# Eleven of 22 gate and up tiles of a ConvGLU from seven products of quarters in place of eight

## The chip, the cores and the metric

The kernel runs on one core of a Trainium2 chip. The metric is the device time of one execution in microseconds; the median of three runs stands for the kernel. Engines are named as in the profile: PE is TensorE's matmul stream and PEld its weight loads, DVE is VectorE, ACT ScalarE, POOL GpSimd, and SP the SyncE queue that issues most of the loads.

## The reference

One encoder layer on 512 tokens of width 1024, all in float32: a mixer of window attention and dilated attention, a cross attention to 256 memory tokens, and a ConvGLU, each followed by a residual and a layer norm. The change lies in the ConvGLU alone:

```python
def conv_glu(h, w_gate, w_up, conv_w, conv_b, w_down):
    s = h.shape[1]
    g = h @ w_gate
    half = CONV_WIDTH // 2
    gp = jnp.pad(g, ((0, 0), (half, half), (0, 0)))
    g = sum(gp[:, j:j + s] * conv_w[j] for j in range(CONV_WIDTH)) + conv_b
    return (jax.nn.gelu(g, approximate=False) * (h @ w_up)) @ w_down
```

`h` is 512 x 1024, `w_gate` and `w_up` are 1024 x 2816, `w_down` is 2816 x 1024, and the convolution is three taps wide along the tokens.

## The kernel before

**Number format.** Every float32 operand of a large product is split into two parts that TensorE takes in one pass each: `hi`, a cast on ScalarE (L134), and `lo = raw - hi`, a subtraction on VectorE (L136). A product is three matmuls: hi by hi, hi by lo, lo by hi (`gemm_fm`, L168).

**Layout of the stage.** The tokens' stream after the second layer norm is turned by TensorE (`to_T`, L202) into `h2T`, a pair (hi, lo) of tiles with the 1024 features on the partitions in eight blocks of 128 and the 512 tokens along the free dimension; a block of 128 tokens is turned at a time. The 2816 features of gate and of up are 22 tiles of 128 (`NF`). For one tile f, `w_cols` (L142) loads a 512 KB slice of 128 weight columns on SP's queue into one of three `raw` buffers and splits it into one of six `hi` and one of six `lo` buffers; `gemm_fm` then runs eight blocks by three matmuls of 128 x 128 weights against 512 tokens, 24 matmuls into one PSUM bank. Gate goes into a `g` tile (two one-bank buffers), up into the first bank of an `s` tile (two two-bank buffers); two further one-bank tiles are `t` and `o`. These are all eight banks.

**Tail of a tile** (L1356 to L1365). The gate is scaled by the middle tap and given its bias (ScalarE, L1357), the two outer taps are added from PSUM shifted by one token (VectorE, L1358 and L1361), then Gelu (ScalarE, L1364) and the product with up out of PSUM (VectorE, L1365), which is stored as `act[:, f, :]`.

**Order.** In the entry (L1323 to L1343) tiles 0 and 1 are computed by halves of the tokens, 256 columns a matmul, around the last two transposes (`pre_gemm`), with TensorE's order written out by hand. From L1345 on, tiles 2 to 21 and the down products are ordered by the framework's scheduler, which sets the order of every engine's instructions when the kernel is built and may bring an instruction forward if its inputs are there. On the other engines it does so in the entry too. The instructions run in that fixed order on each engine.

**Down.** `down_ops` (L1389) splits `act[:, k, :]` into two of the twelve `x` buffers and a row block of `w_down` into a hi and a lo buffer; for each k and each of four token blocks six matmuls accumulate into eight banks.

**Tiles that the change touches outside this stage.** `rc` and `rsn` (L498, L499), 2 KB a partition each, hold the cosines and sines of the rotary embedding, which are last read long before the ConvGLU. The `gb` tag of the weight pool has two buffers of 4 KB a partition, used for the norms' gains.

Of the kernel before, what the change touches and what calls it, by code (L numbers as in the profile page):

```python
# [9 lines left out]
F32 = mybir.dt.float32  # L10
F32R = mybir.dt.float32r
I32 = mybir.dt.int32
AF = mybir.ActivationFunctionType
ALU = mybir.AluOpType
# [3 lines left out]
P = 128  # L18
D = 1024
S = 512  # L20
NB = S // P
KD = D // P
# [3 lines left out]
NF = DFF // P  # L26
# [22 lines left out]
]  # L49

MEM_AT = (2, 0)
WARM = (12, 3)
CI, CF, CS, CMA, CM1, CM3 = 0, 128, 129, 130, 514, 770
CW = 898
# [17 lines left out]
def hymba_layer(ctx: ExitStack, tc: tile.TileContext, A, cst_d, out):  # L72
    nc = tc.nc
    X = mybir.AxisListType.X

    def pool(name, bufs=1, side="left", space=None):
        kw = {} if space is None else {"space": space}
        if space is None:
            kw["side"] = side
        return tc.tile_pool(name=name, bufs=bufs, **kw)  # L80

    cpool = ctx.enter_context(pool("const", side="right"))
    wpool = ctx.enter_context(pool("weights", side="right"))
    spool = ctx.enter_context(pool("small", bufs=3, side="right"))
    xpool = ctx.enter_context(pool("x2k", side="right"))
    spool.tile([P, 32], F32, tag="sfill", bufs=1, name="sfill")
    dpool = ctx.enter_context(tc.tile_pool(name="scratch", bufs=1, space=DRAM))

    cst = cpool.tile([P, CW], F32, name="cst")
    ident = cst[:, CI : CI + P]  # L90
    mhalf = cpool.tile([P, 1], F32, name="mhalf")
# [47 lines left out]
    def wsplit(raw, shape, eng=None):  # L139
        return split(raw, shape, wpool, "hi", 6, wpool, "lo", 6, eng)  # L140

    def w_cols(w, c0, eng=None):  # L142
        raw = wpool.tile([P, KD, P], F32, tag="raw", bufs=3, name="raw")
        nc.sync.dma_start(raw, w.rearrange("(k p) f -> p k f", p=P)[:, :, c0 : c0 + P])
        return wsplit(raw, [P, KD, P], eng)
# [10 lines left out]
    def on_pe(ins):  # L156
        if pe["pin"]:
            pe["pin"] = False
            tc.keep_in_program_order(ins)

    def pin():

        pe["pin"] = True

    def mm(o, l, r, first, last):
        on_pe(nc.tensor.matmul(o, l, r, start=first, stop=last))  # L166

    def gemm_fm(ps, wt, T, c0, n):  # L168
        whi, wlo = wt
        thi, tlo = T  # L170
        for k in range(KD):
            mm(ps, whi[:, k, :], thi[:, k, c0 : c0 + n], k == 0, False)
            mm(ps, whi[:, k, :], tlo[:, k, c0 : c0 + n], False, False)
            mm(ps, wlo[:, k, :], thi[:, k, c0 : c0 + n], False, k == KD - 1)
# [18 lines left out]
    def ps_tile(tag, bufs, shape=None):  # L193
        return gpool.tile(shape or [P, 512], F32, tag=tag, bufs=bufs, name=tag)

    def g_tile():
        return ps_tile("g", 2)

    def s_tile():
        return ps_tile("s", 2, [P, 2, 512])  # L200

    def to_T(t, T, b):  # L202
        ps = s_tile()
        for i in range(KD):
            f = i % 4 * P
            on_pe(nc.tensor.transpose(ps[:, i // 4, f : f + P], t[:, i * P : (i + 1) * P], ident))  # L206
        for i in range(2):
            k = slice(4 * i, 4 * i + 4)
            src = ps[:, i, :].rearrange("p (k t) -> p k t", k=4)
            hi = T[0][:, k, b * P : (b + 1) * P]  # L210
            nc.scalar.copy(hi, src)
            nc.vector.tensor_tensor(T[1][:, k, b * P : (b + 1) * P], src, hi.bitcast(F32), ALU.subtract)

    mid = ExitStack()
    tpool = mid.enter_context(pool("tT"))
# [18 lines left out]
    h = [(oA, oB)[b // 2][:, 2 * (b % 2) : 2 * (b % 2) + 2, :].rearrange("p a f -> p (a f)") for b in range(NB)]  # L234
# [134 lines left out]
    with tc.manual_schedule(engines={nc.tensor.engine, nc.vector.engine, nc.scalar.engine}):  # L369
# [5 lines left out]
        def busy(n, ps=None):  # L375
            for _ in range(n):
                mm((spare if ps is None else ps)[:, 0:P], ones_t, ones_t, True, True)

        busy(WARM[0])
        gps = [g_tile(), g_tile()]  # L380
# [3 lines left out]
        for n in range(2):  # L384
            mm(bt[n], ones_t, rows[:, 1, n, :], True, True)
        busy(WARM[1])
        vps = [g_tile(), g_tile()]
        two = s_tile()
# [106 lines left out]
        hl(3, *all_k)  # L495
        spill(2)

        rc = cpool.tile([P, S], F32, name="rc")  # L498
        rsn = cpool.tile([P, S], F32, name="rsn")  # L499
        posi = zs[:, 0, :].bitcast(I32)  # L500
        nc.sync.dma_start(posi, A["positions"].partition_broadcast(P)[:, 0, :])
        ang = zs[:, 2, :]
# [429 lines left out]
    with tc.manual_schedule(engines={nc.tensor.engine}):  # L932
# [125 lines left out]
        for c in range(KD):  # L1058
            whi, wlo = w_cols(w_xk, c * P)
            done("B2")  # L1060
            ps = g_tile()
# [52 lines left out]
        for hf in range(2):  # L1114
            wts = load_win(hf * 512)
            for b in range(NB):
                ps = g_tile()
# [6 lines left out]
    h = [hp[b] for b in range(NB)]  # L1124
# [28 lines left out]
    def U_pair():  # L1153
        return (
            U.tile([P, KD, S], F32R, tag="Uhi", name="Uhi"),
            U.tile([P, KD, S], F32R, tag="Ulo", name="Ulo"),
        )
# [80 lines left out]
    pin()  # L1238
    with tc.manual_schedule(engines={nc.tensor.engine}):
        to_T(h[0], h1T, 0)  # L1240
        for hf in range(2):
            dil_add(3, hf, dil_mm(3, hf))
        layer_norm(h[3], g1, b1)
        to_T(h[1], h1T, 1)
        proj_xv(1, [ps_tile("t", 1), ps_tile("o", 1)])
        kv(0)
        to_T(h[2], h1T, 2)
        wq = [w_cols(w_xq, c * P) for c in range(4)]
        part = [g_tile(), g_tile(), ps_tile("t", 1)]
# [50 lines left out]
        h2T = U_pair()  # L1300
# [16 lines left out]
    fp = ctx.enter_context(pool("ffn"))  # L1317
# [2 lines left out]
    nc.scalar.dma_start(cw[66:88, :], A["conv_b"][0].rearrange("(c p) -> c p", p=P))  # L1320
    cwT = fp.tile([P, 128], F32, name="cwT")[:, 0:88]
    act = fp.tile([P, NF, S], F32, name="act")
    pre = {}  # L1323
    pin()
    with tc.manual_schedule(engines={nc.tensor.engine}):
        pre = [[None, ps_tile("t", 1)], [None, ps_tile("o", 1)], [None, g_tile()], [None, g_tile()]]

        def pre_gemm(i, s2):
            if s2 == 0:
                pre[i][0] = w_cols(A[("w_gate", "w_up")[i % 2]][0], i // 2 * P)  # L1330
            gemm_fm(pre[i][1][:, s2 * 256 : (s2 + 1) * 256], pre[i][0], h2T, s2 * 256, 256)

        to_T(h[2], h2T, 2)
        pre_gemm(0, 0)
        pre_gemm(1, 0)
        tp = s_tile()[:, 0, 0:88]
        nc.tensor.transpose(tp, cw, ident[0:88, 0:88])
        nc.vector.tensor_copy(cwT, tp)
        pre_gemm(2, 0)
        to_T(h[3], h2T, 3)  # L1340
        pre_gemm(3, 0)
        for i in range(4):
            pre_gemm(i, 1)  # L1343

    pin()  # L1345
    for f in range(NF):
        if f < 2:
            pg, pu = pre[2 * f][1], pre[2 * f + 1][1]
        else:
            wg = w_cols(A["w_gate"][0], f * P)  # L1350
            wu = w_cols(A["w_up"][0], f * P)
            pg = g_tile()
            pu = s_tile()[:, 0, :]
            gemm_fm(pg, wg, h2T, 0, S)
            gemm_fm(pu, wu, h2T, 0, S)
        c = fp.tile([P, S], F32, tag="c", bufs=3, name="c")  # L1356
        nc.scalar.activation(c, pg, AF.Identity, scale=cwT[:, 22 + f : 23 + f], bias=cwT[:, 66 + f : 67 + f])  # L1357
        nc.vector.scalar_tensor_tensor(  # L1358
            c[:, 1:S], pg[:, 0 : S - 1], cwT[:, f : f + 1], c[:, 1:S], ALU.mult, ALU.add
        )  # L1360
        nc.vector.scalar_tensor_tensor(  # L1361
            c[:, 0 : S - 1], pg[:, 1:S], cwT[:, 44 + f : 45 + f], c[:, 0 : S - 1], ALU.mult, ALU.add
        )
        nc.scalar.activation(c, c, AF.Gelu)  # L1364
        nc.vector.tensor_tensor(act[:, f, :], c, pu, ALU.mult)  # L1365
    g3, b3 = (wpool.tile([P, D], F32, tag="gb", bufs=2, name="gb3") for _ in range(2))
    nc.sync.dma_start(g3, A["ln3_g"][0].partition_broadcast(P))
    nc.sync.dma_start(b3, A["ln3_b"][0].partition_broadcast(P))
    with gs:
        acc = [[ps_tile("t", 1), ps_tile("o", 1)]]  # L1370
        for b in range(1, NB):
            two = s_tile() if b != 2 else None
# [16 lines left out]
        def down_ops(k):  # L1389
            w = w_rows(A["w_down"][0], k, 1, 0, D)  # L1390
            a = split(act[:, k, :], [P, S], xpool, "x", 12, xpool, "x", 12)
            return w, a

        for k in range(KO):
            w, a = down_ops(k)
# [48 lines left out]
```

## Time and profile before

| | |
|---|---|
| median of 3 runs | 916.28 us (915.74 to 916.54) |
| the profiled execution | 916.33 us |
| its span, first to last instruction | 914.6 us, so 1.7 us lie around it |
| granted TensorE clock | 0.998 of full speed |
| entry of the ConvGLU (tiles 0 and 1) | about 545 to 571.4 us of the span |
| tiles 2 to 21 | about 571.4 to 787.4 us |
| down products and last norm | about 787.4 to 914.6 us |
| DMA | 92.81 MB, 101 GB/s over the span |

Times in the profile are microseconds from the span's start. A group's row names the line, the engine, the operation, the tile written and the tiles read, and the shape; then the busy time, the mean duration of one in nanoseconds, and the time that the engine was idle just before them with what ended it. Matmuls overlap each other in the records, so the duration of one is longer than the distance from its start to the next one's. L166 is the helper that issues nearly every matmul, so that the tile's name tells the groups apart.

### The profile page before, as it was taken

The numbers are of one execution on the slowest core, as the hardware profiler recorded it, in microseconds if no ns is written. First come the engines' busy times: TensorE is split into PE (matmuls) and PEld (weight loads), VectorE is DVE, ScalarE is ACT, GpSimd is POOL, SyncE is SP. The second block draws the span as 40 slices with busy tenths as digits, with TensorE's granted clock in tenths as the row PEclk, the third lists the DMA queues.
The fourth block names the chain that finished last, engine by engine and source line by source line (L and its number), as shares of the span: only waits on it lengthen the run. The fifth ranks groups of instructions, "written<-read, shape, count | busy, mean of one in ns | idle before, by whom it ended". The sixth has DMA issues, their size and how long they took to land.

```text
span 914.6 us, 12181 instructions
## 1 busy us (share of the span) xinstructions
PE 903.1 (99%) x4809; PEld 760.0 (83%) x4809; DVE 497.2 (54%) x856; ACT 362.3 (40%) x636; POOL 127.5 (14%) x106
## 2 busy tenths in 40 slices
PE   9999999999999999999999999999999999999996
PEld 7778987898878898789988889888888888888885
DVE  7975146435446677778565595543344434333346
ACT  4564436415545476314553224432332333222210
POOL 1064034332444420010000010000000000000001
PEclk9999999999999999999999999999999999999999
DMA  6762041314222338316212314333333332223201
GB/s 218 227 209 72 22 138 48 87 52 116 70 70 58 98 105 249 116 47 184 77 64 68 108 44 150 116 99 108 93 92 92 101 107 92 92 93 98 86 24 70
DMA packets 116940, 92.81 MB, mean 101 GB/s; under 512 B 12472, under 2 KB 100752, under 8 KB 116882
## 3 DMA queue, kind: packets, MB, share of 16 engines
q1 hardware_dynamic: 116048, 89.80, 32.3%
q10 hardware_dynamic: 834, 2.22, 0.6%
q8 instruction: 38, 0.62, 0.3%
q14 instruction: 20, 0.16, 0.1%
HBM read 87.82 MB, written 4.19 MB: 101 GB/s over the span
## 4 chain that ended last, share of the span: by engine, by line
PE 95%; DVE 3%; DMA 1%; issue 0%; ACT 0%; POOL 0%; DVEq 0%; ACTq 0%
PE g L166 53%; PE s L166 27%; PE t L166 4%; PE o L166 4%; PE o L690 3%; PE s L678 2%; PE s L206 1%; DMA vt<-in_ln_in_g_dram 1%; PE s L1221 0%; DVE lo L277 0%; DVE oA L343 0%; DVE st L307 0%; DVE Tlo L362 0%; POOL zs L526 0%; DVE mx L1202 0%
## 5 line engine op out<-in xcount | busy, mean ns | idle before, releaser
L136 DVE TENSOR_TENSOR lo<-raw,hi 128x1024 fp32r<-128x1024 f32 x142 | 176.7, 1246 | 156.9 <-ACT hi L134 154.6
L134 ACT CAST hi<-raw 128x1024 fp32r<-128x1024 f32 x142 | 149.2, 1052 | 221.1 <-PE g L166 163.3
L166 PE MATMUL g<-Thi,hi 128*128 128x512 f32 x240 | 94.8, 395 | 0.0
L166 PE MATMUL g<-Tlo,hi 128*128 128x512 f32 x240 | 94.3, 393 | 0.0
L166 PE MATMUL g<-Thi,lo 128*128 128x512 f32 x240 | 94.0, 392 | 0.0
L166 PE MATMUL g<-Uhi,hi 128*128 128x512 f32 (+1 forms) x256 | 93.2, 364 | 0.0
L166 PE MATMUL g<-Uhi,lo 128*128 128x512 f32 (+1 forms) x256 | 92.8, 363 | 0.0
L166 PE MATMUL g<-Ulo,hi 128*128 128x512 f32 (+1 forms) x256 | 92.8, 363 | 0.0
L107 POOL TENSOR_TENSOR rs<-ve,mhalf 128x1 f32<-128x1 f32 x18 | 15.4, 854 | 530.0 <-DVE ve L113 521.8
L526 POOL TENSOR_TENSOR zs<-zs,rsn 128x512 f32<-128x512 f32 x29 | 59.3, 2046 | 147.1 <-DVE zs L525 147.1
L166 PE MATMUL g<-hi,Thi 128*128 128x512 f32 x184 | 71.6, 399 | 0.0
L166 PE MATMUL g<-hi,Tlo 128*128 128x512 f32 x184 | 71.0, 395 | 0.5 <-DVE Tlo L1169 0.5
L166 PE MATMUL g<-lo,Thi 128*128 128x512 f32 x184 | 70.6, 395 | 0.4 <-DVE lo L277 0.4
L166 PE MATMUL s<-Uhi,lo 128*128 128x512 f32 x160 | 62.3, 389 | 0.0
L166 PE MATMUL s<-Ulo,hi 128*128 128x512 f32 x160 | 62.3, 389 | 0.0
L166 PE MATMUL s<-Uhi,hi 128*128 128x512 f32 x160 | 62.2, 389 | 0.0
L524 DVE TENSOR_TENSOR zs<-g,rc 128x512 f32<-128x512 f32 x29 | 20.0, 688 | 68.1 <-PE g L166 31.5
L166 PEld LDWEIGHTS g<-Uhi,lo 128*128 128x128 f32 x256 | 48.3, 189 | 7.6
L166 PEld LDWEIGHTS g<-Uhi,hi 128*128 128x128 f32 x256 | 48.3, 189 | 7.4
L166 PEld LDWEIGHTS g<-Ulo,hi 128*128 128x128 f32 x256 | 48.2, 188 | 7.4
L166 PEld LDWEIGHTS g<-Thi,hi 128*128 128x128 f32 x240 | 45.1, 188 | 11.0 <-issue 0.9
L166 PEld LDWEIGHTS g<-Tlo,hi 128*128 128x128 f32 x240 | 45.1, 188 | 10.3 <-issue 1.4
(330 smaller groups left out, 1765.3 us busy)
## 6 DMA issues: line engine op xcount, KB each, us to landing
raw<-in_w_in_dram SPq DMA_DIRECT2D x37, 512.0 KB, 3.8
raw<-in_w_gate_dram SPq DMA_DIRECT2D x22, 512.0 KB, 3.8
raw<-in_w_up_dram SPq DMA_DIRECT2D x22, 512.0 KB, 3.9
raw<-in_w_down_dram SPq DMA_DIRECT2D x22, 512.0 KB, 3.3
raw<-in_w_xk_dram SPq DMA_DIRECT2D x8, 512.0 KB, 3.9
raw<-in_w_xv_dram SPq DMA_DIRECT2D x8, 512.0 KB, 3.3
raw<-in_w_xq_dram SPq DMA_DIRECT2D x8, 512.0 KB, 4.8
raw<-in_w_xo_dram SPq DMA_DIRECT2D x8, 512.0 KB, 3.3
```

The lines of the kernel that those rows point to most:

```text
L107: nc.gpsimd.tensor_tensor(out_, in_, mhalf, ALU.pow)
L134: nc.scalar.copy(hi, raw)
L136: (eng or nc.vector).tensor_tensor(lo, raw, hi.bitcast(F32), ALU.subtract)
L166: on_pe(nc.tensor.matmul(o, l, r, start=first, stop=last))
L206: on_pe(nc.tensor.transpose(ps[:, i // 4, f : f + P], t[:, i * P : (i + 1) * P], ident))
L524: nc.vector.tensor_tensor(zc, ps, rc, ALU.mult)
L526: nc.gpsimd.tensor_tensor(sh, sh, rsn, ALU.mult)
L678: nc.tensor.transpose(tp[:, k, :], s_, ident)
L690: nc.tensor.matmul(o[HJ[j], t0:t1], lhs(j), rhs(j), start=i == 0, stop=i == len(parts) - 1)
```

## The change

Take gate and up of one feature tile as a 2 x 2 block product. The weights are cut into four: the upper and lower half of the 1024 input features (four blocks of 128 each) of gate (`a11`, `a12`) and of up (`a21`, `a22`). The tokens' stream is cut into four: the same halves of the features by the left and right 256 tokens (`B11` to `B22`). Eight products of quarters make gate and up; Strassen's method in Winograd's form makes them from seven, with four sums of weight quarters (`s1` to `s4`, made anew for each tile), four sums of stream quarters (`T`, made once), and additions of the products behind them. The tiles in `SEVEN` are made in this way, the others as before. TensorE's order is written out by hand for all of tiles 0 to 21.

```diff
+SEVEN = (4, 5, 7, 8, 10, 11, 13, 14, 16, 17, 19)
...
+    rope = [cpool.tile([P, S], F32, tag="rope", bufs=2, name=n) for n in ("rc", "rsn")]
...
-    def to_T(t, T, b):
+    def to_T(t, T, b, raw=None):
...
+            if raw is not None:
+                nc.scalar.copy(raw[:, k, b * P : (b + 1) * P], src)
...
-        rc = cpool.tile([P, S], F32, name="rc")
-        rsn = cpool.tile([P, S], F32, name="rsn")
+        rc, rsn = rope
...
+    raw_u = act[:, NF - KD : NF, :]
...
-        to_T(h[2], h2T, 2)
+        to_T(h[2], h2T, 2, raw_u)
...
-        to_T(h[3], h2T, 3)
+        to_T(h[3], h2T, 3, raw_u)
...
+    def t_form(n, i, a, b):
+        k = slice(2 * i, 2 * i + 2)
+        r = act[:, 6 + 2 * n : 8 + 2 * n, :].rearrange("p a (b t) -> p (a b) t", t=HT)
+        nc.vector.tensor_tensor(r[:, k], a[:, k], b[:, k], ALU.subtract)
+        if n < 3:
+            hl = [xpool.tile([P, 2, HT], F32R, tag="x", bufs=12, name="x") for _ in range(2)]
+        else:
+            hl = [t4[:, 2 * i : 2 * i + 2, :], cpool.tile([P, 2, HT], F32R, tag="rope", bufs=2, name="t4l")]
+        nc.scalar.copy(hl[0], r[:, k])
+        nc.vector.tensor_tensor(hl[1], r[:, k], hl[0].bitcast(F32), ALU.subtract)
+        T.setdefault(n, []).append(hl)
+        T["raw", n] = r
+    def t_forms():
+        for r, q in ((R11, B11), (R21, B21)):
+            nc.vector.tensor_tensor(r, q[0].bitcast(F32), q[1].bitcast(F32), ALU.add)
+        for n, a, b in ((0, R12, R11), (2, R22, R12), (1, R22, 0), (3, R21, 1)):
+            for i in range(2):
+                t_form(n, i, a, b if n in (0, 2) else T["raw", b])
...
+    def product(ps, wt, u):
+        for k in range(HK):
+            for a, b in ((0, 0), (0, 1), (1, 0)):
+                mm(ps, wt[a][:, k, :], u(b, k), k + a + b == 0, k == HK - 1 and a == 1)
+    def parts(raw, n):
+        hi = wpool.tile([P, n, P], F32R, tag="hi", bufs=6, name="hi")
+        nc.scalar.copy(hi, raw)
+        lo = wpool.tile([P, n, P], F32R, tag="lo", bufs=6, name="lo")
+        nc.vector.tensor_tensor(lo, raw, hi.bitcast(F32), ALU.subtract)
+        return [[t[:, HK * i : HK * (i + 1), :] for t in (hi, lo)] for i in range(n // HK)]
+    def seven(f):
...
+        s13, s24 = (wpool.tile([P, KD, P], F32, tag="gb", bufs=2, name="gb") for _ in range(2))
...
+        A11, A12 = parts(raw[0], KD)
+        nc.vector.tensor_tensor(s1, a21, a22, ALU.add)
+        nc.vector.tensor_tensor(s3, a11, a21, ALU.subtract)
+        S1, S3 = parts(s13, KD)
+        nc.vector.tensor_tensor(s2, s1, a11, ALU.subtract)
+        nc.vector.tensor_tensor(s4, a12, s2, ALU.subtract)
+        S2, S4 = parts(s24, KD)
+        (A22,) = parts(a22, HK)
+        p1_ = ps_tile(("t", "o")[f % 2], 1)[:, sl]
+        product(p1_, A11, quarter(B11))
+        two = [g_tile(), g_tile(), s_tile()[:, 0, :]]
+        product(two[0][:, sl], A12, quarter(B21))
+        product(two[1][:, sl], S1, moving(0))
+        product(two[1][:, sr], S3, moving(2))
+        product(two[0][:, sr], S2, moving(1))
+        product(two[2][:, sl], S4, quarter(B22))
+        product(two[2][:, sr], A22, moving(3))
+        gu = fp.tile([P, 2 * S], F32, tag="gu", bufs=1, name="gu")
+        u34 = act[:, f, :]
...
+        nc.scalar.copy(gu[:, S + HT :], p1_)
+        nc.vector.tensor_tensor(pair(gu[:, 0:S]), pair(two[0]), twice(gu[:, S + HT :]), ALU.add)
+        nc.vector.tensor_tensor(pair(u34), pair(two[1]), twice(gu[:, sr]), ALU.add)
+        nc.vector.tensor_tensor(gu[:, S + HT :], two[1][:, sl], u34[:, sr], ALU.add)
+        nc.vector.tensor_tensor(gu[:, HT : S + HT], two[2], u34, ALU.add)
+        ffn_tail(f, gu[:, 0:S], gu[:, S:])
+    pin()
+    with tc.manual_schedule(engines={nc.tensor.engine}):
+        t_forms()
+        for f in range(2):
+            ffn_tail(f, pre[2 * f][1], pre[2 * f + 1][1])
+        for f in range(2, NF):
+            if f in SEVEN:
+                seven(f)
+                continue
...
+            gemm_fm(pg, wg, h2T, 0, S)
+            gemm_fm(pu, wu, h2T, 0, S)
+            ffn_tail(f, pg, pu)
```

`HT` is 256 tokens and `HK` four blocks of 128 features; `sl` and `sr` are the left and right half of 512 columns. `ffn_tail` is the tail of a tile as it was (L1356 to L1365), in a function. The raw right half of the stream is copied out of PSUM in `to_T` into tiles 14 to 21 of `act`, the left half is put together again as hi + lo, and the raw differences lie in tiles 6 to 13 of `act`; all of these are done with before the tiles are written. `gu`, 4 KB a partition with one buffer, holds gate and up of a changed tile for the tail. `moving` and `quarter` pick the hi or lo part of a difference or of a quarter of `h2T`.

More of the change, by code (lines that the diff above doesn't have):

```diff
@@ L1343, in hymba_layer, with ffn_tail @@
             pre_gemm(i, 1)
[L1345 to L1355, printed above, removed]
+    def ffn_tail(f, pg, pu):
         c = fp.tile([P, S], F32, tag="c", bufs=3, name="c")
@@ L1365, in hymba_layer @@
         nc.vector.tensor_tensor(act[:, f, :], c, pu, ALU.mult)
+    HT, HK = S // 2, KD // 2
+    sl, sr = slice(0, HT), slice(HT, S)
+    B11, B12, B21, B22 = (
+        [t[:, HK * i : HK * (i + 1), n] for t in h2T] for i in range(2) for n in (sl, sr)
+    )
+    R11, R12, R21, R22 = (raw_u[:, HK * i : HK * (i + 1), n] for i in range(2) for n in (sl, sr))
+    T = {}
+    t4 = fp.tile([P, HK, HT], F32R, name="t4")
+    def t_form(n, i, a, b):
[10 more added lines that the diff above has]
+        T["raw", n] = r
@@ new lines, in t_forms, with moving, quarter @@
+    def t_forms():
[4 more added lines that the diff above has]
+                t_form(n, i, a, b if n in (0, 2) else T["raw", b])
+    def moving(n):
+        return lambda w, k: T[n][k // 2][w][:, k % 2, :]
+    def quarter(q):
+        return lambda w, k: q[w][:, k, :]
+    def product(ps, wt, u):
+        for k in range(HK):
+            for a, b in ((0, 0), (0, 1), (1, 0)):
+                mm(ps, wt[a][:, k, :], u(b, k), k + a + b == 0, k == HK - 1 and a == 1)
@@ new lines, in parts, with twice, pair @@
+    def parts(raw, n):
[5 more added lines that the diff above has]
+    def seven(f):
+        raw = []
+        for name in ("w_gate", "w_up"):
+            raw.append(wpool.tile([P, KD, P], F32, tag="raw", bufs=3, name="raw"))
+            nc.sync.dma_start(raw[-1], A[name][0].rearrange("(k p) f -> p k f", p=P)[:, :, f * P : (f + 1) * P])
+        a11, a12, a21, a22 = (t[:, HK * i : HK * (i + 1), :] for t in raw for i in range(2))
+        s13, s24 = (wpool.tile([P, KD, P], F32, tag="gb", bufs=2, name="gb") for _ in range(2))
+        s1, s3, s2, s4 = (t[:, HK * i : HK * (i + 1), :] for t in (s13, s24) for i in range(2))
+        A11, A12 = parts(raw[0], KD)
[17 more added lines that the diff above has]
+        u34 = act[:, f, :]
+        def twice(v):
+            return v.unsqueeze(1).to_broadcast([P, 2, HT])
+        def pair(v):
+            return v.rearrange("p (a t) -> p a t", a=2)
+        nc.scalar.copy(gu[:, S + HT :], p1_)
[4 more added lines that the diff above has]
+        ffn_tail(f, gu[:, 0:S], gu[:, S:])
@@ new lines, in hymba_layer @@
+    pin()
[7 more added lines that the diff above has]
+                continue
+            wg = w_cols(A["w_gate"][0], f * P)
+            wu = w_cols(A["w_up"][0], f * P)
+            pg = g_tile()
+            pu = s_tile()[:, 0, :]
+            gemm_fm(pg, wg, h2T, 0, S)
+            gemm_fm(pu, wu, h2T, 0, S)
+            ffn_tail(f, pg, pu)
```

## The prediction

> **What bounds the kernel now.** I read the page's first part, then the chain that ended last, then the busy time by stage, then the groups of the gate and up stage, shapes kept apart.
>
> ```profile
> PE 903.1 (99%) x4809; PEld 760.0 (83%) x4809; DVE 497.2 (54%) x856; ACT 362.3 (40%) x636; POOL 127.5 (14%) x106
> PE 95%; DVE 3%; DMA 1%; issue 0%; ACT 0%; POOL 0%; DVEq 0%; ACTq 0%
> ```
>
> TensorE holds 95% of the chain. A busy PE is not yet PE at its limit, so the stage that the change rewrites has to be looked at by itself. Two rows of busy time, the first the stretch in which the last two half-width products of the entry run, the second the stage from about feature tile 4 to 21 (duration; busy PE, PEld, DVE, ACT, POOL with instruction counts; granted clock; DMA share; GB/s):
>
> ```profile
> 565.70:571.20 5.50, 5.50 (x48) 5.50 (x47) 4.28 (x6) 5.09 (x6) 0.00 (x0) 1.00 0.64 189
> 593.00:787.30 194.30, 194.30 (x859) 160.90 (x858) 83.31 (x93) 62.88 (x76) 0.00 (x0) 1.00 0.33 99
> ```
>
> In the second, TensorE has no idle time at all at a granted clock of 1.00, VectorE works 83.31 of 194.30 us, ScalarE 62.88. So a microsecond of matmul removed here is a microsecond of the kernel, as long as VectorE and ScalarE can carry what is put on them. What a matmul costs I take from the chain, since it gives the time of a whole run of back-to-back matmuls:
>
> ```profile
> 565.76 5.76 PE g L166 x48
> 571.52 6.15 PE s L166 x27
> 577.67 10.88 PE g L166 x48
> ...
> 596.93 5.44 PE s L166 x24
> 602.37 5.44 PE g L166 x24
> ```
>
> The first row is 48 matmuls of 256 columns (the second halves of feature tile 1's gate and up): 5.76/48 = 0.120 us each. The others have 512 columns: 5.44/24 = 0.2267 us each. Half the columns cost 53%, not 50%: 0.0133 us of each matmul does not shrink with its width. That is the whole price of Strassen's smaller blocks on TensorE.
>
> The groups' own durations must not be used for this:
>
> ```profile
> L166 PE MATMUL g<-Uhi,hi 128*128 128x512 f32 x192 | 74.8, 390 | 0.0
> L166 PE MATMUL g<-Uhi,hi 128*128 128x256 f32 x64 | 18.4, 287 | 0.0
> ```
>
> At 390 and 287 ns a tile would go from 48 x 0.390 = 18.7 us to 84 x 0.287 = 24.1 us; but 48 matmuls of 287 ns fit in 5.76 us only because they overlap, so these are latencies. The Trainium skill says the same of matmul rows ("Perfetto Trace Analysis", Identifying the Most-Contended Engine: pipelined matmuls make busy time a bad measure; the share of weight loading is the better one), and by that measure the half-width stretch is full, PEld 5.50 of 5.50 us, where the full-width stage has 160.90 of 194.30.
>
> **The change, TensorE.** An ordinary tile has gate and up, 2 x 24 matmuls of 512 columns: 2 x 5.44 = 10.88 us. A changed tile has seven products of 4 x 3 = 12 matmuls of 256 columns: 84 x 0.120 = 10.08 us. Difference 0.80 us, eleven times: **-8.8 us**. Seven eighths would have given 1.36 us per tile; the width takes 0.56 of it back.
>
> Here a rule stands beside the row. The Trainium skill ("TensorE: Matmul & The Clock Gate", Back-to-back issue gap) gives a warm gap of N/2.4 + 2.5 ns, 109.2 ns at 256 and 215.8 ns at 512 columns; by it a tile would save 48 x 0.2158 - 84 x 0.1092 = 1.19 us and the change 13.0 us. The trace has both widths in the same loop, at 0.120 and 0.2267 us, so I use 8.8.
>
> **VectorE and ScalarE per tile.** Groups of VectorE in the stage (busy us, mean ns, idle time before and what ended it), then one of the whole kernel for the 256-column shape, then ScalarE's of the whole kernel:
>
> ```profile
> L136 DVE TENSOR_TENSOR lo<-raw,hi 128x1024 fp32r<-128x1024 f32 x36 | 44.1, 1225 | 74.2 <-ACT hi L134 72.5
> L1361 DVE SCALAR_TENSOR_TENSOR c<-g,cwT,c 128x511 f32<-128x511 f32 x18 | 13.5, 750 | 0.6
> L1358 DVE SCALAR_TENSOR_TENSOR c<-g,cwT,c 128x511 f32<-128x511 f32 x18 | 13.4, 744 | 0.0
> L1365 DVE TENSOR_TENSOR act<-c,s 128x512 f32<-128x512 f32 x18 | 12.4, 688 | 33.6 <-PE s L166 33.6
> L136 DVE TENSOR_TENSOR lo<-act,hi 128x512 fp32r<-128x512 f32 x3 | 2.1, 685 | 0.7 <-ACT hi L134 0.7
> ```
> ```profile
> L905 DVE TENSOR_TENSOR x<-s,x 128x256 fp32r<-128x256 f32 x8 | 3.4, 419 | 1.8 <-ACT x L904 1.8
> ```
> ```profile
> L134 ACT CAST hi<-raw 128x1024 fp32r<-128x1024 f32 x142 | 149.2, 1052 | 221.1 <-PE g L166 163.3 <-PE s L166 26.8 <-issue 6.9
> L1357 ACT ACTIVATE c<-g,cwT 128x512 f32<-128x512 f32 x21 | 16.3, 777 | 0.0
> L1364 ACT ACTIVATE c<-c 128x512 f32<-128x512 f32 x22 | 13.9, 632 | 41.2 <-DVE c L1361 41.2
> L134 ACT CAST hi<-act 128x512 fp32r<-128x512 f32 x22 | 13.7, 622 | 63.4 <-PE s L166 62.4 <-DVE act L1365 1.0
> ...
> L1067 ACT COPY kmT<-g 128x256 f32<-128x256 f32 x8 | 2.9, 367 | 0.0
> ```
>
> An ordinary tile on VectorE: two lows 2 x 1.225, tail 0.744 + 0.750 + 0.688: **4.63 us**. A changed tile: four sums of quarters, 128x512, at 0.685 = 2.74; lows 3 x 1.225 + 0.685 = 4.36; the recombination, three of 512 and one of 256 out of PSUM, 3 x 0.688 + 0.419 = 2.48; the same tail, 2.18: **11.76 us**, more than the tile's 10.08 us of TensorE. On ScalarE it is 3 x 1.052 + 0.622 + 0.367 + 0.777 + 0.632 = 5.55 us, no bound.
>
> So VectorE is the question. The eleven tiles come in five pairs (4 5, 7 8, 10 11, 13 14, 16 17), each followed by an ordinary tile, and 19 alone. Over such a three VectorE has 2 x 11.76 + 4.63 = 28.2 us of durations, TensorE 2 x 10.08 + 10.88 = 31.04 us: 91%. It is less in truth, because starts are closer than durations:
>
> ```profile
> 563.92 1.23 DVE L136 TENSOR_TENSOR lo<-raw,hi 128x1024 fp32r<-128x1024 f32 x1 [5.96 <-ACT hi L134]
> ...
> 570.84 0.74 DVE L1358 SCALAR_TENSOR_TENSOR c<-g,cwT,c 128x511 f32<-128x511 f32 x1
> 571.50 0.68 DVE L136 TENSOR_TENSOR lo<-act,hi 128x512 fp32r<-128x512 f32 x1
> 572.10 0.74 DVE L1361 SCALAR_TENSOR_TENSOR c<-g,cwT,c 128x511 f32<-128x511 f32 x1
> 572.76 1.21 DVE L136 TENSOR_TENSOR lo<-raw,hi 128x1024 fp32r<-128x1024 f32 x1
> ```
>
> From 571.50 to 572.10 is 0.60 us for an instruction of 0.68; with some 0.08 us less on each of 16 instructions a changed tile is near 10.5 us and a three near 25 us, about 82%. It fits if VectorE forms weights ahead of the pair. Six hi and lo buffers serve: a changed tile takes four and frees the first after its second product. Counting through a three, every set can be formed 11 us or more before its product (the ordinary tile's gate set: freed at 8.64 us of the three, needed at 20.16). That is the cover under which I cost the eleven weight formations at nothing. Bounds: nothing at one end, at the other the full excess of an uncovered pair, 2 x (11.76 - 10.08) = 3.4 us. I take nothing, since the pitch row is the nearer one.
>
> The raw weights are the same bytes, two loads a tile on SP's queue, but each of the three raw buffers is held until the last sum of quarters has read it, and the next tile's load waits in SP's queue behind it. The latest load (a pair's second up tile) comes some 8 us ahead of its use; a load lands in:
>
> ```profile
> raw<-in_w_gate_dram SPq DMA_DIRECT2D x22, 512.0 KB, 3.8
> ```
>
> so that wait is covered too, cost nothing; without cover it would be 3.8 us once a pair.
>
> **PSUM and the single recombination buffer.** A changed tile holds both g buffers. Its first (products 2 and 5) is wanted by an ordinary tile 2.88 us after product 5 ends (products 6 and 7), by another changed tile 4.32 us after. Freeing it takes one 0.688 us add, and that needs the copy of product 1 in gu, which has one buffer: the tail of the changed tile before must be through. From that tile's end: 0.69 + 0.78 + 0.74 + 0.75 + 0.63 + 0.69 for the tail, 0.37 and 0.69 for copy and add, 5.3 us where 10.08 are there before the ordinary tile needs the buffer. Behind each waiting step VectorE's later weight formations queue, and behind the g buffer all of TensorE, whose order is now by hand. Four VectorE steps that each find a 1.23 us formation under way make 10.3 us: a stall of 0.2 us in each pair. Zero to 1.0 us in all, I take **+0.5**.
>
> **The entry.** New at the start are four PSUM copies, two sums of 1024, eight differences and eight lows of 512 and eight casts: on VectorE 2 x 1.225 + 16 x 0.685 = 13.4 us, from when the last transpose is split. The timeline above shows VectorE idle 5.96 us before 563.92, and seven(4) does not need them until some 24 us after tile 2's start; by themselves they are hidden. But they stand ahead of the tails of tiles 0 and 1, and tile 2's gate needs a g buffer that tile 1's tail frees. Before, the scheduler could run up tiles first (the chain's 27 s matmuls, then 48 g), and eight of them even earlier, from the first to the last of these rows but one:
>
> ```profile
> 558.10 0.40 PE L166 MATMUL s<-Uhi,hi 128*128 128x512 f32 x1
> ...
> 561.17 0.39 PE L166 MATMUL s<-Ulo,hi 128*128 128x512 f32 x1
> ...
> 571.36 0.40 PE L166 MATMUL s<-Uhi,lo 128*128 128x512 f32 x1
> ```
>
> By hand the gate comes first. Without these eight the entry ends at 571.36 - 8 x 0.2267 = 569.5 us, tile 1's gate at 566.8. Before, its buffer came free 4.2 us after the gate's end (568.6 to 572.10 + 0.74 = 572.84); at the same delay that is 571.0 now, a stall of 1.5 us.
>
> Ends: zero if the tail is prompt, 3.6 us if all 13.4 us go first. I take **+1.5**. Of the copies, one can stand in ScalarE's queue ahead of the second split of the last transpose:
>
> ```profile
> L211 ACT CAST Uhi<-s 128x512 fp32r<-128x512 f32 x16 | 9.3, 585 | 48.6 <-PE s L206 46.6 <-DVE Ulo L212 1.9
> ```
> ```profile
> 557.27 0.69 DVE L212 TENSOR_TENSOR Ulo<-s,Uhi 128x512 fp32r<-128x512 f32 x1 [0.65 <-ACT Uhi L211]
> ```
>
> That split ends at 557.96; 0.59 later is 558.55, and its four row blocks are read twelve half-width matmuls after 557.98, at 559.4. Cost nothing, at worst 0.6. None of these edits can give time below nothing: in this stage TensorE has no idle time to win back.
>
> **The exit.** All twelve x buffers hold differences until tile 19 is through, so the splits of act for the down stage cannot run early (before, the first was at 571.50). Two ordinary tiles, 21.8 us of TensorE, follow tile 19, and VectorE needs 9.3 us of them: cost nothing; without that cover one cast and low, 1.3 us, once.
>
> **Sum.** The profiled execution took 916.33 us (span 914.6), against the median of 916.28. 916.33 - 8.8 + 1.5 + 0.5 = **909.5 us**.
>
> **Rivals.** *No stall at all*: 907.5. For it, the idle VectorE of the stage; against it, the tile 2 gate. It is the low side of my case.
>
> *VectorE sets the pace in each pair.* Its order is fixed ahead and in order; where a recombination that waits for a product stands before the next tile's formations, nothing is formed ahead and the pair takes VectorE's 11.76 us a tile: 5 x 3.4 + 1.7 = 18.7 us of stalls more than TensorE's time, 916.33 - 8.8 + 1.5 + 18.7 = 927.7, slower. For it, the durations; against it, the pitch, and the ordinary tile's lows before, which waited for buffers, not for VectorE's turn (idle 74.2 us). It decides from 7.3 us of stalls in the pairs, 0.7 us a changed tile, and is clear from 9.1. Chance 0.15.
>
> *The cover holds in part*: 0.3 to 0.8 us of stall a changed tile on top of 909.0 (the sum without the 0.5), 912 to 918. Chance 0.22, half of it still clearly faster.
>
> *The narrow matmuls lose their fixed part*, 0.1133 us each, half of 0.2267: 1.36 us a tile, 15.0 in all, 916.33 - 15.0 + 2.0 = 903.3. The row of 48 matmuls speaks against it: 0.03. The Trainium skill's gap rule named above would lie between, at 905.3.
>
> *The entry blocks for its full 3.6 us*: 911.6, inside my case. That the change does not do what it says would show in the count of matmuls, which should grow by 11 x 36 = 396.
>
> **Chances.** About 0.2% (1.8 us) is what can be told from no change here: faster is below 914.5, slower above 918.1. My case (907 to 912) has 0.60, the cheaper narrow matmuls 0.03, half of the partial cover 0.11: faster 0.74. Same 0.11, slower 0.15. The range leaves out the pace-setting VectorE and the cheaper matmuls: 906.8 to 917.0.
>
> **What would show it.** Right: half-width products at 0.120 us start to start, changed tiles of 10.1 us in the chain, 5205 matmuls, VectorE over 80% busy in the stage, a gap of 1 to 3 us ahead of tile 2's gate, hardly any in the pairs. Wrong: TensorE waiting ahead of a g product on the recombination or the tail, or on a low of a weight sum; or a pitch off 0.120.

## The result, and the profile after

The changed kernel is slower, by 0.7%: **922.75 us** (922.01 to 923.18, 6 runs) against 916.29 us (915.74 to 916.68, 6 runs), ratio 1.007 with a 95% interval of 1.0057 to 1.0083. Forecast were 909.5 us and a range of 906.8 to 917.0.

The page's first part, then the shares of the chain that ended last:

```profile
span 921.1 us, 13178 instructions
PE 897.6 (97%) x5205; PEld 772.9 (84%) x5205; DVE 578.3 (63%) x984; ACT 392.0 (43%) x681; POOL 127.2 (14%) x106
PE 84%; DVE 9%; DMA 3%; issue 2%; ACT 1%; POOL 0%; SPq 0%; DVEq 0%; ACTq 0%
```

There are 396 more matmuls, as they should be, and TensorE is busy 5.5 us less. But its share of the chain fell from 95 to 84%, and VectorE's rose from 3 to 9%: TensorE now waits. The chain of the changed kernel (start, duration, group), from the layer norm behind the entry to the end of the first pair:

```profile
521.67 16.32 PE g L168 x72
544.27 2.35 DVE lo L138 x2
563.06 1.91 DVE act L1376 x4
578.88 7.32 PE g L168 x24
586.20 5.44 PE s L168 x24
...
602.51 1.43 PE t L168 x12
603.95 5.76 PE g L168 x48
609.71 2.88 PE s L168 x24
612.59 1.44 PE o L168 x12
614.03 5.76 PE g L168 x48
619.79 1.45 PE s L168 x12
623.10 5.73 PE g L168 x24
```

The products cost what was forecast: 48 half-width matmuls in 5.76 us, and tile 4 runs from 602.51 to 612.59, 10.08 us. The losses are around them: the chain leaves TensorE for VectorE from 544 to 578.88 us, tile 2's gate takes 7.32 us in place of 5.44, and the ordinary tile behind the pair starts at 623.10, though the pair's last matmul started at 622.38. The waits of TensorE name the rest (waiting instruction, releaser: us in total, times, longest):

```profile
PE g L168 <- DVE c L1355: 6.5, 1, 6.5
PE g L168 <- DVE gu L1447: 2.8, 5, 0.7
PE s L208 <- DVE h L126: 1.8, 1, 1.8
```

L1355 is the last tap of a tile's tail, here tile 1's; L1447 the add that frees a changed tile's first g buffer; L126 the layer norm ahead of the last transposes. Measured from start to start of the matmuls on either side, less their pace, these are 6.7, 3.6 (five of about 0.7) and 2.0 us.

A fourth loss is in no list of waits. TensorE's matmuls around the end of the long one:

```profile
578.88 0.77 PE L168 MATMUL g<-Uhi,hi 128*128 128x512 f32 x1 [6.51 <-DVE c L1355]
579.44 0.63 PE L168 MATMUL g<-Ulo,hi 128*128 128x512 f32 x1
579.87 0.63 PE L168 MATMUL g<-Uhi,lo 128*128 128x512 f32 x1
...
582.36 0.40 PE L168 MATMUL g<-Uhi,lo 128*128 128x512 f32 x1
582.59 0.40 PE L168 MATMUL g<-Uhi,hi 128*128 128x512 f32 x1
```

Behind the wait they start 0.43 us apart, and from 582.36 on 0.23 again: 3.48 us for eight starts that take 1.81 at full pace, 1.7 us lost. Busy time by stage shows why, in its clock column (third from the end), in the wait, behind it, after that, and, fourth, in one stretch of two changed tiles and an ordinary one:

```profile
572.00:578.80 6.80, 0.36 (x4) 0.16 (x2) 6.80 (x12) 2.96 (x3) 0.00 (x0) 0.75 0.27 77
578.80:582.50 3.70, 3.62 (x9) 2.94 (x10) 2.26 (x3) 0.63 (x1) 0.00 (x0) 0.53 0.18 45
582.50:590.00 7.50, 7.50 (x35) 6.17 (x34) 4.20 (x6) 1.73 (x2) 0.00 (x0) 1.00 0.16 48
...
623.10:654.89 31.79, 31.32 (x216) 29.21 (x216) 26.29 (x36) 14.63 (x19) 0.00 (x0) 1.00 0.35 100
```

The clock fell to about half while TensorE waited (0.75 is the mean of the whole wait), was still there for some 3.5 us behind it, and rose again. In the last row VectorE is busy 26.29 of 31.79 us, near the 25 that the prediction reckoned with: it is not the bound of this kernel.

Together: -8.8 + 2.0 + 6.7 + 1.7 + 3.6 = +5.2 us of the 6.5 measured. Of the other 1.3, 0.9 was there before the ConvGLU (the 72 matmuls at 521.67 us stood at 520.80). In the experiments' traces the same matmuls start anywhere from 519.98 to 522.46, in a part that the change leaves as it was; what shifts it was not tried. From these 72 matmuls to the last group of the chain that writes `t` (at 890.69 us before, 897.20 now), which leaves this shift out, the change costs 5.6 us.

**What held the tap.** VectorE's instructions in the entry of the changed kernel (start, duration):

```profile
548.88 1.22 DVE L1389 TENSOR_TENSOR act<-Uhi,Ulo 128x1024 f32<-128x1024 f32 x1
...
550.61 1.22 DVE L1389 TENSOR_TENSOR act<-Uhi,Ulo 128x1024 f32<-128x1024 f32 x1
551.74 0.69 DVE L131 BATCH_NORM_STATS2 st<-h 128x6 f32<-128x512 f32 x1
...
568.34 0.74 DVE L1352 SCALAR_TENSOR_TENSOR c<-t,cwT,c 128x511 f32<-128x511 f32 x1
...
572.53 0.74 DVE L1355 SCALAR_TENSOR_TENSOR c<-t,cwT,c 128x511 f32<-128x511 f32 x1
...
573.79 0.68 DVE L1421 TENSOR_TENSOR gb<-raw 128x512 f32<-128x512 f32 x1
574.40 1.21 DVE L1409 TENSOR_TENSOR lo<-raw,hi 128x1024 fp32r<-128x1024 f32 x1
575.53 0.68 DVE L1422 TENSOR_TENSOR gb<-raw 128x512 f32<-128x512 f32 x1
576.13 0.74 DVE L1352 SCALAR_TENSOR_TENSOR c<-g,cwT,c 128x511 f32<-128x511 f32 x1
...
577.39 0.68 DVE L1424 TENSOR_TENSOR gb<-gb,raw 128x512 f32<-128x512 f32 x1
577.99 0.74 DVE L1355 SCALAR_TENSOR_TENSOR c<-g,cwT,c 128x511 f32<-128x511 f32 x1
```

Both sums of the left half (L1389) need only the first two blocks of the stream, and the scheduler put them ahead of the last block's layer norm (L131 and what follows): 2.4 us of VectorE, 2.0 us of TensorE. Then the differences and lows of the quarter sums, and behind them sums and lows of tile 4's weights (L1421 to L1424), needed some 25 us later, stand ahead of tile 1's taps (L1352 at 576.13, L1355 at 577.99). These four instructions take 2.9 us from start to start (573.79 to 576.13 and 577.39 to 577.99); an estimate from these rows is that the quarter sums alone would have made a wait of some 3.8 us.

### The profile page after: what moved, and what is told of

Same layout as the page of the kernel before. It is cut to its first block, busy times and chain, and to the rows that moved or that the text cites. A ratio compares the mean times of both kernels' runs of the same rounds, so it can differ in the third digit from the quotient of the medians.

```text
span 921.1 us, 13178 instructions
## 1 busy us (share of the span) xinstructions
PE 897.6 (97%) x5205; PEld 772.9 (84%) x5205; DVE 578.3 (63%) x984; ACT 392.0 (43%) x681; POOL 127.2 (14%) x106
## 4 chain that ended last, share of the span: by engine, by line
PE 84%; DVE 9%; DMA 3%; issue 2%; ACT 1%; POOL 0%; SPq 0%; DVEq 0%; ACTq 0%
PE g L168 49%; PE s L168 20%; PE t L168 5%; PE o L168 4%; PE o L693 3%; PE s L681 2%; DMA raw<-in_w_mix_out_dram 2%; DVE lo L138 1%; DMA raw<-in_w_up_dram 1%; DVE lo L1409 1%; PE s L208 1%; DMA vt<-in_ln_in_g_dram 1%; ACT hi L136 1%; DVE Ulo L214 1%; DVE act L1376 0%
## 5 line engine op out<-in xcount | busy, mean ns | idle before, releaser
L138 DVE TENSOR_TENSOR lo<-raw,hi 128x1024 fp32r<-128x1024 f32 x120 | 149.8, 1251 | 79.5 <-ACT hi L136 78.7
L136 ACT CAST hi<-raw 128x1024 fp32r<-128x1024 f32 x120 | 125.9, 1050 | 138.3 <-PE g L168 86.6
L168 PE MATMUL g<-Uhi,hi 128*128 128x256 f32 (+1 forms) x212 | 72.9, 344 | 9.3 <-DVE c L1355 6.5
L168 PE MATMUL g<-x,hi 128*128 128x256 f32 x392 | 71.8, 284 | 0.0
L168 PE MATMUL g<-Ulo,hi 128*128 128x256 f32 (+1 forms) x212 | 71.7, 338 | 0.0
L168 PE MATMUL g<-Uhi,lo 128*128 128x256 f32 (+1 forms) x212 | 71.6, 338 | 0.0
L168 PEld LDWEIGHTS g<-x,hi 128*128 128x128 f32 x392 | 61.2, 192 | 0.5 <-issue 0.3
L168 PE MATMUL g<-x,lo 128*128 128x256 f32 x196 | 55.5, 283 | 0.0
L168 PEld LDWEIGHTS g<-Thi,lo 128*128 128x128 f32 x240 | 45.1, 188 | 9.3
L138 DVE TENSOR_TENSOR lo<-act,hi 128x512 fp32r<-128x512 f32 x22 | 14.8, 689 | 52.8 <-ACT hi L136 52.8
```

The lines of the kernel that those rows point to most:

```text
L136: nc.scalar.copy(hi, raw)
L138: (eng or nc.vector).tensor_tensor(lo, raw, hi.bitcast(F32), ALU.subtract)
```

## The experiments

The kernel before ran beside them at 916.33 us (order_only, one_tile, after_tails, gu2), 916.44 (up_first, all_mended, sixteen, filler) and 916.13 (split_sums, twelve, all_mended_again). Two theories were held against each other: **entry and buffer** (the losses are the four above, made by the order of VectorE's work at the entry and by the one recombination buffer) and **load** (VectorE's work in the changed tiles sets the pace).

**order_only.** No changed tile, no quarter sums.

```diff
-SEVEN = (4, 5, 7, 8, 10, 11, 13, 14, 16, 17, 19)
+SEVEN = ()
...
-        t_forms()
```

> No changed tile and no sums of stream quarters: what is left of the change is TensorE's order by hand for tiles 2 to 21 and the four PSUM copies. Entry theory (the stall of 6.7 us ahead of tile 2's gate comes from the quarter sums that stand ahead of the tails of tiles 0 and 1 in VectorE's queue): with them gone the gate waits 0 to 1.5 us, 916.3 to 918.0 us. Rival (the order by hand makes the wait, since the scheduler may no longer put up tiles first): the full 6.7 us and the slow matmuls behind it, about 924 us.

918.04 us (916.73 to 918.56), ratio 1.0017 (1.0007 to 1.0026). The one wait on the last tap is 1.5 us:

```profile
PE g L168 <- DVE c L1355: 1.5, 1, 1.5
```

So the order by hand, with the four PSUM copies, costs 1.6 us by itself, start to start. The rest of the 6.7 comes from what this run leaves out: the quarter sums, and with the changed tiles also the sums and lows of tile 4's weights. This run doesn't tell the two apart.

**one_tile.** All quarter sums, but only tile 4 is changed.

```diff
-SEVEN = (4, 5, 7, 8, 10, 11, 13, 14, 16, 17, 19)
+SEVEN = (4,)
```

> Only tile 4 is changed, so all sums of stream quarters are made but there is no pair. Entry theory: the whole entry cost is there (2.0 us ahead of the last transpose, 6.7 ahead of tile 2's gate, 1.7 of slow matmuls behind it, 10.4 together) and one tile's gain of 0.8: about 926 us, slower than with eleven changed tiles. Rival (VectorE's load in the eleven tiles is what costs): 10/11 of the loss goes, about 916 us.

926.15 us (925.9 to 926.47), ratio 1.0108 (1.0093 to 1.0123): 3.4 us slower than with all eleven. In its trace the waits on the tap and the layer norm are as long as in the changed kernel's, 6.5 and 1.8 us, and there is none on the recombination. As the cause of this kernel's loss, load in the changed tiles has fallen.

**after_tails.** VectorE's part of the quarter sums is issued behind tile 1's last tap.

```diff
+            tap = ffn_tail(f, pre[2 * f][1], pre[2 * f + 1][1])
+        with tc.issue_after(tap.ins):
+            t_forms()
```

> All eleven tiles, but VectorE's part of the quarter sums is issued behind the last tap of tile 1 (an edge of issue order, no wait). Entry theory: the 2.0, 6.7 and 1.7 us go, 922.75 - 10.4 = 912.3 us, up to 914 if a shorter wait stays at tile 2's gate; if the sums now come late for tile 4, a new wait at its third product shows. Rival (load in the pairs): about 922 us, the waits move into the tiles.

917.73 us (917.06 to 918.96), ratio 1.0018 (1.0009 to 1.0027): 5.0 us are won, not 10.4. The wait on the layer norm is gone (0.2 us left), that on the tap is still 4.1:

```profile
PE g L168 <- DVE c L1355: 4.1, 1, 4.1
PE g L168 <- DVE gu L1448: 2.6, 5, 0.6
PE s L208 <- DVE h L126: 0.2, 1, 0.2
```

Now tile 4's weight sums and lows, without the quarter sums, stood ahead of the taps: from 567.52 to 572.85 us VectorE had six of them and one tap. The theory was right about the layer norm and half right about the tap: other work of the changed tiles took the place of the quarter sums ahead of it. Behind the wait of 4.1 us the clock was at 0.50 of full speed for 5.3 us.

**gu2.** A second place for the recombination buffer.

```diff
+        if SEVEN.index(f) % 2:
+            gu = act[:, NF - 2 :, :].rearrange("p a t -> p (a t)")
+        else:
+            gu = fp.tile([P, 2 * S], F32, tag="gu", bufs=1, name="gu")
```

> All eleven tiles as in the changed kernel, but the recombination buffer has a second place (the space of tiles 20 and 21 of act) used by every second changed tile. Buffer theory (the wait of 0.6 to 0.9 us behind each of five pairs is the add waiting for the one gu buffer): the five waits go, 922.75 - 3.6 = 919.1 us. Rival (the add waits for its turn in VectorE's queue behind weight formations): the waits stay, 922 to 922.75 us.

918.48 us (917.56 to 919.28), ratio 1.0024 (1.0014 to 1.0035), 4.3 us less than the changed kernel. No wait on the recombination is left; those on the tap (5.4) and the layer norm (1.8) stay. How one buffer made them shows in VectorE's order behind a pair's first tile in the changed kernel:

```profile
679.35 0.75 DVE L1355 SCALAR_TENSOR_TENSOR c<-gu,cwT,c 128x511 f32<-128x511 f32 x1
680.79 0.69 DVE L1421 TENSOR_TENSOR gb<-raw 128x512 f32<-128x512 f32 x1 [0.69 <-DMA raw<-in_w_up_dram]
681.40 1.22 DVE L1409 TENSOR_TENSOR lo<-raw,hi 128x1024 fp32r<-128x1024 f32 x1
682.54 0.68 DVE L1422 TENSOR_TENSOR gb<-raw 128x512 f32<-128x512 f32 x1
683.14 0.68 DVE L1424 TENSOR_TENSOR gb<-gb,raw 128x512 f32<-128x512 f32 x1
683.74 0.68 DVE L1359 TENSOR_TENSOR act<-c,gu 128x512 f32<-128x512 f32 x1
...
686.08 0.68 DVE L1447 TENSOR_TENSOR gu<-g,gu 128x512 f32<-128x512 f32 x1
```

The tail's last product (L1359) frees gu. Its Gelu ended at 680.83, but it runs at 683.74: ahead of it stand four weight formations, and the first waits for a load of raw weights.

**up_first.** In tile 2, up ahead of gate in TensorE's order.

```diff
+            two = [(pg, wg), (pu, wu)]
+            for ps, wt in two[::-1] if f == 2 else two:
+                gemm_fm(ps, wt, h2T, 0, S)
```

> All eleven tiles, and in tile 2 the up product runs ahead of the gate in TensorE's order; nothing else is moved. If the wait at tile 2's gate is for tile 1's last tap, 5.44 us of other matmuls now cover it: 6.7 us shrink to about 1.2 and the 1.7 us of slow matmuls go, 922.75 - 7.2 = 915.5 us. If TensorE waits at that place for something else (the quarter sums themselves, or weights), the wait comes back at the up product: about 922 us.

915.47 us (914.47 to 916.03), ratio 0.9987 (0.9977 to 0.9996), 7.3 us less than the changed kernel. The wait on the tap and the slow matmuls behind it are gone, with nothing done to VectorE's work: TensorE has something else to do there. In this run's trace the dozen matmuls behind the layer norm's wait are slow instead: the work there takes 1.5 us more than in the changed kernel's trace (last section). The layer norm and the recombination still cost their parts:

```profile
PE g L168 <- DVE gu L1447: 3.4, 5, 1.2
PE s L208 <- DVE h L126: 1.8, 1, 1.8
```

**all_mended.** The last three edits together.

> Three edits together: quarter sums issued behind the last tap of tile 1, tile 2's up product first, second place for the recombination buffer. Entry and buffer theory: no wait over 0.5 us is left, 922.75 - 2.0 - 6.7 - 1.7 - 3.6 = 908.7 us, the 8.8 us that the matmuls save less about one. Rival (VectorE's load sets the pace once the other waits are gone): waits of 1 to 2 us come back in every pair, 915 us or more.

909.06 us (908.66 to 909.72), ratio 0.9918 (0.9903 to 0.9933); a second time 909.29 us, 0.9921 (0.9908 to 0.9935):

> The kernel with three edits again, beside the two that follow from it: 909 us, within half a microsecond.

One wait is left, in tile 4, where the late quarter sums hold tile 3's last tap:

```profile
PE g L168 <- DVE c L1355: 1.6, 1, 1.6
```

**split_sums.** The first half of the quarter sums goes back into VectorE's idle time behind the last transpose.

```diff
+        with tc.issue_after(low.ins):
+            t_forms(0)
         for f in range(2):
             tap = ffn_tail(f, pre[2 * f][1], pre[2 * f + 1][1])
         with tc.issue_after(tap.ins):
+            t_forms(1)
```

> The kernel with three edits, but the first half of the quarter sums (both sums of 1024, differences 0 and 2) is issued behind the split of the last transpose, in VectorE's idle time there, and only the second half behind the last tap of tile 1. The one wait left in the kernel with three edits (1.7 us in tile 4, on tile 3's last tap) is theirs if it is made by the late quarter sums: 909.06 - 1.7 = 907.4 us. If the early half pushes tile 1's taps back past the cover of 5.44 us, a wait of 1 to 2 us returns at tile 2's gate: about 909 us.

**908.02 us** (907.57 to 908.39), ratio 0.9909 (0.9895 to 0.9922). The trace lists no wait of TensorE from the entry to the down stage; 8.1 of the 8.8 us have arrived, 8.3 without the shift ahead of the ConvGLU (from the 72 matmuls to the last group on `t`).

**sixteen.** The kernel with three edits, tiles 4 to 19 all changed.

> As the kernel with all three edits, but all of tiles 4 to 19 are made from seven products, with no ordinary tile between them. VectorE is busy 26.3 us in a stretch of two changed tiles and one ordinary in the changed kernel's trace, so about 10.9 us a changed tile, against 10.08 of TensorE. If VectorE sets the pace when nothing gives it room: up to 16 x 0.9 = 14 us of waits, less what it forms ahead, 912 to 918 us. If TensorE keeps the pace: 908.7 - 5 x 0.8 = 904.7 us.

913.86 us (912.94 to 915.95), ratio 0.9975 (0.9964 to 0.9986): 4.8 us slower than all_mended with five more tiles changed. Two stretches:

```profile
625.00:655.00 30.00, 28.97 (x242) 28.79 (x241) 29.49 (x43) 15.36 (x21) 0.00 (x0) 1.00 0.36 104
685.00:715.00 30.00, 28.97 (x242) 28.80 (x241) 29.83 (x44) 14.65 (x20) 0.00 (x0) 1.00 0.31 88
```

VectorE is busy 29.5 to 29.8 of 30 us, TensorE 28.97. TensorE waits once in every two tiles, for a cast of weight sums (L1408) or an add of the recombination (L1453), and two changed tiles take 21.3 to 21.7 us in place of 20.16. This is the load theory's kernel: the mechanism of the slower rival exists, and the ordinary tiles between the changed ones are what keeps it away.

**twelve.** As split_sums, with four threes of changed tiles, each before an ordinary one.

> As split_sums, but twelve changed tiles in four threes (4 to 6, 8 to 10, 12 to 14, 16 to 18), each followed by an ordinary one. VectorE has 3 x 10.9 + 4.4 = 37.1 us where TensorE has 3 x 10.08 + 10.88 = 41.1: if only the mean over a stretch matters, 0.8 us less than split_sums, 906.6 us. If VectorE must keep up within a three, it falls 3 x 0.8 us behind and part of it shows as waits at the g buffer: 908 to 911 us.

**907.25 us** (906.26 to 907.34), ratio 0.9898 (0.9885 to 0.9912), the fastest, 0.8 us below split_sums as the mean over a stretch would have it. The two intervals overlap, but the one trace of each agrees: from the 72 matmuls to the last group on `t` it has 360.6 us and split_sums 361.6. In 41 us TensorE has no idle time and VectorE 4.0 us:

```profile
636.00:677.00 41.00, 41.00 (x302) 39.11 (x301) 37.03 (x50) 19.75 (x25) 0.00 (x0) 1.00 0.36 104
```

**filler.** The changed kernel with 24 matmuls into an unread PSUM half ahead of tile 2's gate.

```diff
+        idle = s_tile()[:, 1, :]
+        for k in range(24):
+            mm(idle, pre[3][0][0][:, k % KD, :], h2T[0][:, k % KD, :], True, True)
```

> The changed kernel with 24 matmuls of 512 columns ahead of tile 2's gate, into half of a PSUM tile that nobody reads: 5.4 us of TensorE's work inside the wait of 6.7. If the eight matmuls of 0.43 us behind that wait are slow because TensorE stood idle, they run at 0.227 now: 922.75 - 1.7 = 921.0 us. If they are slow for another reason: 922.75 us. If the fillers delay the rest: up to 5.4 us more.

924.31 us (921.8 to 924.74), ratio 1.0078 (1.0063 to 1.0093), against 921.0 expected. At its place the expectation held: the gate starts at 578.18 and its matmuls follow each other at full pace. But the pairs came out otherwise, with waits of 5.4 us on the recombination in place of 2.8, and behind the longest the slow pace again:

```profile
654.75 0.79 PE L168 MATMUL g<-Uhi,hi 128*128 128x512 f32 x1 [2.44 <-DVE gu L1447]
655.35 0.63 PE L168 MATMUL g<-Ulo,hi 128*128 128x512 f32 x1
655.77 0.63 PE L168 MATMUL g<-Uhi,lo 128*128 128x512 f32 x1
```

That standing idle makes the slow pace at tile 2's gate is shown, here and in up_first; the total says nothing of it. Why the waits in the pairs grew was not tried.

## Why the prediction was wrong, point by point

**The matmuls**: right. 0.120 us at half width, 10.08 us a tile, and -8.1 us in the kernel without waits (split_sums), where 8.8 were forecast. The gap of the Trainium skill ("TensorE: Matmul & The Clock Gate", Back-to-back issue gap, where it is given for an isolated matmul), 13.0 us in this sum, is not borne out by any of these runs.

**VectorE per tile**: right. 26.3 us busy in a three against "near 25" and at most 28.2. (The working counts 16 VectorE instructions in a changed tile where its own list has 15; that makes 10.6 us in place of 10.5.) The kernel did become slower, but not in the way of the slower rival. sixteen shows that rival's mechanism in another choice of tiles, at 0.6 to 0.8 us a changed tile where it had 1.7.

**The entry**: this step failed. It took +1.5 us, with 3.6 as the far end; it was 2.0 + 6.7 + 1.7 = 10.4, shown by one_tile, which has little else. The 1.5 was right for what it was derived from, the order by hand (1.6 in order_only). The rest came from three things that the step left out. First, it let the new work start "from when the last transpose is split"; two sums did not need that transpose and went ahead of the layer norm, which was then on the path with no room. Second, the bound of 3.6 us counted the quarter sums alone ahead of the taps, and for these it was nearly right (the estimate above is 3.8); sums and lows of tile 4's weights went there too, and with them alone ahead the gate still waited 4.2 us (after_tails). Third, a wait was priced at its length, without what TensorE's clock does after it.

**The recombination buffer**: the chain and its place were right (the ordinary tile behind each pair), the size was not, 3.6 us against 0.5 taken and 1.0 as its bound. It allowed one formation ahead of each step; ahead of a single step stood four, of which one waited for a load. So the raw loads, costed at nothing since they come in time for their products, still cost as a wait in the middle of VectorE's queue.

**The exit**: nothing, as forecast; from the last gate or up matmul to the end it is 127.6 us in both traces.

## What to carry to other kernels

Where one engine paces the kernel and another gets new work, a mean load below the pacing engine's is needed (sixteen lacked it) but is not enough: list what stands ahead of each instruction that frees a buffer for the pacing engine, work that is needed much later included, and ask which new instructions could run earlier than their place in the text. The wait of the pacing engine was covered more cheaply here on that engine, by doing first what has its buffer (up_first won 7.3 us by the order of two products), than by hurrying the one waited for (after_tails won 5.0). And a change that lost by its edges is worth taking apart: the products here saved nearly what they promised, and with their edges mended the kernel is 0.9 to 1.0% faster than before.

## What the runs showed of the hardware that was not expected

TensorE's clock can fall to half behind a wait of a few microseconds. Behind waits of 6.7 us (the changed kernel), 4.2 (after_tails) and 2.6 (filler), from start to start, matmuls of 512 columns began 0.43 us apart for about 3.5 us or more, at a granted clock of 0.50 to 0.53. Behind waits of 1.6 us (order_only) and 1.7 (all_mended) they did not. The wait of 2.0 us for the layer norm went both ways. In the traces of the changed kernel, one_tile and filler the matmuls of 256 columns behind it kept their 0.12 us; in those of gu2 and up_first, with the same work at that place, they began 0.21 us apart until about 560 us. Busy time just behind that wait, first in the changed kernel, then in gu2:

```profile
557.60:560.00 2.40, 2.40 (x23) 2.40 (x22) 0.72 (x2) 1.24 (x3) 0.00 (x0) 1.00 0.00 0
557.60:560.00 2.40, 2.40 (x13) 2.40 (x13) 1.10 (x2) 1.61 (x3) 0.00 (x0) 0.50 0.00 0
```

So there is no safe length to be read off between 1.7 and 2.6 us; what decides at 2.0 no run here shows. The Trainium skill ("TensorE: Matmul & The Clock Gate", Part 1) has an activity window of about 3.4 us, after an idle one of which the clock is at half; the cases of 2.6 and 2.0 us are shorter than that.
